# Grouped-query layer: four weight subtractions ordered behind the norm's last root, and the first attention pair written ahead of the second query projection

## The chip, the cores and the metric

The kernel runs on one core of a Trainium2 chip. The metric is the device time of one execution in microseconds (us). Before the change it is 1528.57 us, the median of three runs (1526.31 to 1530.88).

## The reference, cut to what matters

Two blocks follow one another on 256 tokens of width 1024, all in float32. The first block is two hybrid layers. The second is two transformer layers with a mixture of experts each; its first layer uses neighbourhood attention, its second grouped-query attention with 16 query heads and 4 key/value heads of width 64. The change touches the border between the two layers of the second block and the attention of the second:

```python
for i in range(DEPTH):                       # DEPTH = 2
    sh1, sc1, g1, sh2, sc2, g2 = split(silu(c) @ ada_w[i] + ada_b[i])
    h = x * (1 + sc1) + sh1
    y = neighbourhood_mixer(...) if i == 0 else gqa_mixer(h, ...)
    x = layer_norm(ALPHA * x + (1 + g1) * y, ln_g[i, 0], ln_b[i, 0])
    h = x * (1 + sc2) + sh2
    y = hierarchical_moe(h, ...)             # 32 experts
    x = layer_norm(ALPHA * x + (1 + g2) * y, ln_g[i, 1], ln_b[i, 1])

# gqa_mixer
qkv = h @ w_qkv                              # 1024 x (1024 + 256 + 256)
q, k = rope(rms_norm(q)), rope(rms_norm(k))
o = softmax(q @ k.T * HEAD_DIM**-0.5) @ v    # per head
return o @ w_o
```

## The kernel before, in words

The 256 tokens are two tiles of 128 partitions. A projection multiplies in float32 by splitting both operands into a high part and a remainder: `split` (L116) casts a piece of the weight to the high part on ScalarE (`S.copy`, L124) and subtracts it on VectorE (L125), 1024 columns at a time, and `mm3` (L172) issues three matmuls, high by high, low by high and high by low (L174). A 512-column weight slice takes four casts and four subtractions. Two such split slices of 256 columns are held at a time. In `proj_wide` (L311) with a `feed`, `feed(0)` writes the transposed, scaled activations of token tile 0, the weight is split, and the matmuls of tile 0 run; then `feed(1)` and tile 1. `feeder` (L278) makes one `feed`: per half of the width four transposes of x (L156), four scaled copies out of PSUM that alternate between VectorE (L221) and ScalarE (L227), one cast (L289) and one subtraction (L290).

At the end of the first mixture of experts (`moe` with l = 0, L1216 to L1220), each token tile is normalized: `norm_stats` (L748) takes `bn_stats` of the two halves (L754), the aggregate (L755), and an inverse square root out of small one-column VectorE steps (`rsqrt1`, L202, lines L205 to L209), and ends with L758, the bias of the normalization. `normalize` (L761) then writes the right half of x on ScalarE (L762) and the left half on VectorE (L763), both from PSUM. The 512 key and value columns (`wkv`) of the grouped-query layer have been loaded by then, and their splits need nothing of the norm.

`gqa_layer` (L880) is written in this order: load `wkv` and the first query columns `wq0`; project keys and values (L944, with the feed); load the second query columns `wq1`; project `wq0` (L948); `chain` for the keys (norm and rotation, L949); transpose keys; `chain` for query heads 0 to 7 (L957); project `wq1` (L958); `q_trans(0)`, the transposes of query heads 0 to 7 (L959); `chain` for heads 8 to 15 (L960); load the rows of the expert norm (`ln_rows`); and the loop over eight pairs of heads (L966), with `q_trans(1)` after pair 1 and the affine part of the norm (`affine`, L825) after pairs 3 and 5. `full_heads` (L389) of a pair is: scores into PSUM (tag pd, L393), maximum on VectorE (L345), four exponentials on ScalarE (L356), scaling by the sums (L219, L225), transposes (L156), copies (L217, L223), the product with the values (L398) and the split of the result (L836, L837). Pairs 0 to 3 need query heads 0 to 7 only. Between all this `ada` loads the modulation weights in chunks of 2 MB (L702) and multiplies them (L711, tile pf, 16 records a chunk); block 9 holds one of these chunks first and the softmax tiles later. After the loop come the last chunks, `flush`, and `mixer_out` (L765), whose weights `w_o` are split by the same helper.

PSUM tiles of tag pd (projections and scores) have two buffers, of tag ps three. Weights go through three rotating SBUF blocks; SP issues the loads in its own queue, each when its block is free.

The order of instructions on each engine is fixed when the program is built. A planner plays the program on a simulated timeline, and gives each engine, of the instructions that are ready there, the one written earliest. So the written order is a priority and not the order of execution. `tc.issue_after(i)` adds an edge of order alone: what is traced inside it on the engine of i is queued behind i.

Of the kernel before, what the change touches and what calls it, by code (L numbers as in the profile page):

```python
# [31 lines left out]
def tile_hybrid_then_moe(ctx: ExitStack, tc: tile.TileContext, p: dict, out: bass.AP):  # L32
# [33 lines left out]
    def block(i, dt=F32):  # L66
        i = role.get(i, i)
        t = big[i].tile([128, 4096], dt, name=f"b{i}", tag=f"b{i}")
        return t
# [20 lines left out]
    def cyc(vs):  # L90
        i = [0]

        def nxt():
            i[0] += 1
            return vs[(i[0] - 1) % len(vs)]
        return nxt
# [15 lines left out]
    def splitter():  # L112
        hs, ls = block(3, F32R), block(4, F32R)
        par = [0]

        def split(v):  # L116
            k, n = v.shape[1], v.shape[2]
            o = par[0] * 2048
            par[0] ^= 1
            hi, lo = [a[:, o:o + k * n].rearrange("p (k n) -> p k n", k=k) for a in (hs, ls)]  # L120
            step = max(1, 1024 // n)
            for a in range(0, k, step):
                s = slice(a, min(a + step, k))
                S.copy(hi[:, s], v[:, s])  # L124
                V.tensor_tensor(lo[:, s], v[:, s], hi[:, s].bitcast(F32), OP.subtract)  # L125
            return [(hi[:, a], lo[:, a]) for a in range(k)]
        return split

# [3 lines left out]
    def pair(i):  # L132
        return carve(block(i, F32R), (8, 256), (8, 256))
# [174 lines left out]
                    k == 0, k == 7)  # L308
        return ps.rearrange("p (f t) -> p f t", f=2)

    def proj_wide(h, split, v, feed=None, rest=None, ahead=()):  # L311
        o = PS2()
        if feed:
            feed(0)
            if rest:
                rest()
            with ExitStack() as q:
                for i in ahead:
                    q.enter_context(tc.issue_after(i))
                s = [(a, split(v[:, :, a:min(a + 256, v.shape[2])]))  # L320
                     for a in range(0, v.shape[2], 256)]
            for t in range(2):
                if t:
                    feed(1)
                for a, w in s:
                    proj_tok(h, w, t, o[:, t, a:min(a + 256, v.shape[2])])
            return o
        for a in range(0, v.shape[2], 256):
            n = min(256, v.shape[2] - a)
            s = split(v[:, :, a:a + n])  # L330
            for t in range(2):
                proj_tok(h, s, t, o[:, t, a:a + n])
        return o
# [414 lines left out]
    def norm_stats(src):  # L748
        n = len(src)
        st = small([128, n, 6], f"lst{n}")  # L750
        mv = small([128, 2], "lmv")
        rr = small([128, 2], "lrr")
        for i, v in enumerate(src):
            V.bn_stats(st[:, i], v)  # L754
        V.bn_aggr(mv, st)  # L755
        V.tensor_scalar(rr[:, 1:2], mv[:, 1:2], 1e-5, None, op0=OP.add)
        rsqrt1(rr[:, 0:1], rr[:, 1:2])
        V.tensor_scalar(rr[:, 1:2], mv[:, 0:1], rr[:, 0:1], -1.0, op0=OP.mult, op1=OP.mult)  # L758
        return mv, rr

    def normalize(t, src, mv, rr):  # L761
        S.activation(x[:, t, 512:D], src[1], AF.Identity, scale=rr[:, 0:1], bias=rr[:, 1:2])  # L762
        V.tensor_scalar(x[:, t, 0:512], src[0], mv[:, 0:1], rr[:, 0:1], op0=OP.subtract, op1=OP.mult)  # L763

    def mixer_out(split, l, y, w_o):  # L765
# [114 lines left out]
    def gqa_layer(l, split):  # L880
# [20 lines left out]
        def chain(pw, h0, n, qk):  # L901
            pv = pw[:, :, :n * 64].rearrange("p t (h d) -> p t h d", h=n)
            q = qs[:, :, :n]
            S.activation(q, pv, AF.Square)
            V.tensor_reduce(ssq[:, :, h0:h0 + n], q, AX.X, OP.add)
            rt = small([128, 2, n], f"rt{n}")
            rstd(rt, ssq[:, :, h0:h0 + n], 1e-6, (ALL, 1.0 / 64))
            if qk == 0:
                S.copy(q, pv)
                V.tensor_scalar(rs8[:, h0:h0 + n], rt.rearrange("p t h -> p h t"), 0.125, None, op0=OP.mult)  # L910
            else:
                V.tensor_tensor(q, pv, rt[:, :, :, None].to_broadcast([128, 2, n, 64]), OP.mult)
                S.copy(vv, pw[:, :, 256:512])
            for t in range(2):
                xv = q[:, t].rearrange("p h (a b r) -> p h a b r", a=2, b=2)
                tb = [tab[:, qk, t, i][:, None].to_broadcast([128, n, 2, 16]) for i in range(4)]
                tm = [ro[:, i, :n] for i in range(4)]
                V.tensor_tensor(tm[0], xv[:, :, :, 0], tb[0], OP.mult)
                V.tensor_tensor(tm[1], xv[:, :, :, 1], tb[1], OP.mult)
                V.tensor_tensor(tm[2], xv[:, :, :, 1], tb[2], OP.mult)  # L920
                V.tensor_tensor(tm[3], xv[:, :, :, 0], tb[3], OP.mult)
                for d in ([qk_t[:, t]] if qk == 0 else [kdup[:, t, :, dd] for dd in range(2)]):
                    d = d.rearrange("p h (a b r) -> p h a b r", a=2, b=2)
                    V.tensor_tensor(d[:, :, :, 0], tm[0], tm[1], OP.subtract)
                    V.tensor_tensor(d[:, :, :, 1], tm[2], tm[3], OP.add)

        def q_trans(half):
            for hp in range(2):
                ps = PS()
                for j in range(2):  # L930
                    for t in range(2):
                        hh = 4 * hp + 2 * j
                        tr(ps[:, j * 256 + t * 128:j * 256 + t * 128 + 128],
                           qk_t[:, t, hh:hh + 2].rearrange("p h d -> p (h d)"))
                evac(qT[:, 4 * half + 2 * hp:4 * half + 2 * hp + 2].rearrange("p h t -> p (h t)"), ps)
# [5 lines left out]
            pin[0] = False  # L941
            ada()

        pkv = proj_wide(hT, split, wkv, feed, rest)  # L944
        ada()
        wq1 = cols(wq, 512, 512)
        ada()
# [2 lines left out]
        for hp in range(2):  # L950
# [4 lines left out]
                       kdup[:, t, 2 * hp + j].rearrange("p c d -> p (c d)"))  # L955
            evac(kT[:, 2 * hp:2 * hp + 2].rearrange("p h t -> p (h t)"), ps)
        chain(pq, 0, 8, 0)  # L957
        pq = proj_wide(hT, split, wq1)  # L958
        q_trans(0)  # L959
        chain(pq, 8, 8, 0)  # L960
        lgb = carve(b10[:, 1024:3072], (D,), (D,))
        ln_rows(lgb, 0, 1)
        oT = pair(6)
        s0, s1, t0, t1 = carve(block(9), *[(2, 512)] * 4)
        bufs = (cyc([s0, s1]), cyc([t0, t1]))
        for hp in range(8):  # L966
            kv = hp // 2
            full_heads(bufs, qT[:, hp], kT[:, kv], lambda j: vv[:, :, kv * 64:kv * 64 + 64],
                       rs8[:, 2 * hp:2 * hp + 2], None, put_o(oT, hp))
            if hp == 1:  # L970
                q_trans(1)
            if hp in (3, 5):
                affine(lgb, V, (hp // 4,))
        adab[0] = cyc([7, 2])
        ada(48)
        flush()
# [4 lines left out]
    def moe(l, w1, lg, fs, fb, new):  # L981
# [234 lines left out]
        if not l:  # L1216
            for t in range(2):
                ys = [Y[t][:, 0], Y[t][:, 1]]
                normalize(t, ys, *norm_stats(ys))
            return  # L1220
        st, mv, rr, nm = carve(P.rearrange("p t e s -> p (t e s)"), (2, 2, 6), (2, 2), (2,), (1,))
        h = [slice(0, 512), slice(512, D)]
# [148 lines left out]
```

## Time and profile before

| | us |
|---|---|
| median of three runs | 1528.57 |
| the profiled execution | 1528.28 |
| its span, first to last instruction | 1526.4 |
| TensorE busy (PE) | 1213.0 (79%) |
| VectorE busy (DVE) | 576.3 (38%) |
| ScalarE busy (ACT) | 352.5 (23%) |
| DMA | 532.20 MB, mean 349 GB/s |

Times in the trace count from the span's start. PE is the matmul stream of TensorE, PEld its weight loads, SPq the queue of DMA issues. In a timeline row stand the start, the length, engine, line, operation, output and input tiles, count, and in brackets how long the engine had been idle and what released it. The table of stretches gives busy time per engine, then the granted clock of TensorE as a share of full speed, and the share of the DMA engines' time in use.

### The profile page before, as it was taken

To read this page: it belongs to the slowest core of one execution; us is meant where nothing else is said; L and a number is where in the kernel's file an instruction comes from. 1 tells how busy PE (TensorE), PEld (TensorE's weight loads), DVE (VectorE), ACT (ScalarE), POOL (GpSimd) and SP (SyncE) were. 2 spreads that over 40 slices of the span, in tenths; PEclk is the share of its full clock that TensorE was granted. 3 is DMA by queue.
4 is the path that set the end of the run, shared out by engine and by line. 5 is a ranking of instruction groups with operands and counts; after the bars stand their busy time and mean duration, and the time that the engine had idled before them with its cause. 6 is when DMAs were issued, how large, how long until landed. Compare 5 with 4: busy or idle time off the path is not lost.

```text
span 1526.4 us, 23782 instructions
## 1 busy us (share of the span) xinstructions
PE 1213.0 (79%) x10200; PEld 763.6 (50%) x10200; DVE 576.3 (38%) x1383; ACT 352.5 (23%) x747; POOL 47.9 (3%) x83
## 2 busy tenths in 40 slices
PE   6999899999998896672886677898897774596765
PEld 6887788786766442321432325657443321243322
DVE  6885687556566210100110106867311100011103
ACT  5443445345441010000010004562011000011000
POOL 0000000000000200000000000000300000000000
PEclk9999899999989998876998889899899977799788
DMA  9538444768477999999999999775999999999995
GB/s 360 219 124 336 173 157 159 297 259 349 184 282 291 429 430 430 429 429 430 430 429 430 430 428 381 280 276 212 378 428 431 428 429 430 430 428 430 430 430 211
DMA packets 46557, 532.20 MB, mean 349 GB/s; under 512 B 7024, under 2 KB 10224, under 8 KB 14960
## 3 DMA queue, kind: packets, MB, share of 16 engines
q1 hardware_dynamic: 45296, 527.48, 83.7%
q10 hardware_dynamic: 1152, 3.15, 0.5%
q8 instruction: 82, 1.34, 0.3%
q14 instruction: 27, 0.22, 0.0%
HBM read 529.56 MB, written 1.05 MB: 348 GB/s over the span
## 4 chain that ended last, share of the span: by engine, by line
DMA 46%; PE 43%; DVE 7%; ACT 3%; issue 1%; SPq 0%; DVEq 0%; ACTq 0%
DMA b<-in_moe_w_gate_up_dram 27%; DMA b<-in_moe_w_down_dram 17%; PE ps L159 13%; PE ps L174 11%; PE pd L174 11%; PE pd L159 3%; PE pf L159 3%; PE ps L156 2%; DVE b L125 2%; DMA b<-in_na_bias_dram 1%; ACT b L356 1%; ACT b L124 1%; DMA b<-in_w_in_dram 1%; DVE diag L744 0%; DVE b L868 0%
## 5 line engine op out<-in xcount | busy, mean ns | idle before, releaser
L159 PE MATMUL ps<-b,b 128*32 128x256 f32 (+2 forms) x5248 | 483.3, 476 | 191.0 <-DMA b<-in_moe_w_gate_up_dram 127.1
L159 PEld LDWEIGHTS ps<-b,b 128*32 128x32 f32 (+1 forms) x5248 | 191.5, 120 | 428.8 <-issue 270.1
L174 PE MATMUL ps<-b,b 128*128 128x256 f32 (+1 forms) x1464 | 195.4, 293 | 1.5 <-DVE b L125 1.3
L174 PE MATMUL pd<-b,b 128*128 128x256 f32 (+2 forms) x1152 | 188.0, 321 | 5.7 <-DVE b L464 4.0
L174 PEld LDWEIGHTS ps<-b,b 128*128 128x128 f32 x1464 | 183.9, 192 | 12.1 <-issue 3.2
L174 PEld LDWEIGHTS pd<-b,b 128*128 128x128 f32 x1152 | 163.4, 197 | 31.5 <-issue 7.1
L125 DVE TENSOR_TENSOR b<-b,b 128x1024 fp32r<-128x1024 f32 (+1 forms) x124 | 148.6, 1207 | 74.8 <-ACT b L124 74.3
L124 ACT CAST b<-b 128x1024 fp32r<-128x1024 f32 (+1 forms) x124 | 126.5, 1035 | 152.7 <-PE ps L174 68.9
L223 ACT COPY b<-ps 128x256 f32<-128x256 f32 (+1 forms) x81 | 36.0, 448 | 451.3 <-PE ps L159 305.9
L217 DVE COPY b<-ps 128x256 f32<-128x256 f32 (+1 forms) x71 | 36.1, 508 | 238.1 <-PE ps L159 201.3
L156 PE MATMUL ps<-cst,b 128*128 128x128 f32 (+1 forms) x404 | 76.1, 299 | 41.3 <-DVE b L217 17.5
L1087 DVE SCALAR_TENSOR_TENSOR sl<-sl,ps 128x128 f32<-128x128 f32 x64 | 18.4, 288 | 236.8 <-ACT sl L1086 236.8
L156 PEld LDWEIGHTS ps<-cst,b 128*128 128x128 f32 (+1 forms) x404 | 44.6, 145 | 108.0 <-DVE b L217 34.4
L1135 DVE TENSOR_TENSOR b<-ps,parts 128x512 f32<-128x512 f32 x32 | 22.1, 691 | 190.6 <-PE ps L159 189.5
L159 PE MATMUL pd<-b 64*128 64x512 f32 (+1 forms) x384 | 82.7, 553 | 13.2 <-DVE b L1135 8.3
L159 PEld LDWEIGHTS ps<-b,x 128*128 128x128 f32 x512 | 62.8, 202 | 20.8 <-issue 15.7
L159 PE MATMUL ps<-b,x 128*128 128x128 f32 x512 | 67.1, 290 | 3.7 <-DVE b L1101 1.6
L1086 ACT ACTIVATE sl<-ps 128x128 f32<-128x128 f32 x64 | 17.7, 277 | 222.9 <-PE ps L156 222.9
L1105 POOL TENSOR_TENSOR b<-b,g 128x128 f32<-128x128 f32 x64 | 23.5, 399 | 1249.1 <-DVE b L1101 730.8
L159 PEld LDWEIGHTS pd<-b 64*128 64x128 f32 x384 | 34.6, 192 | 50.1 <-issue 24.0
L227 ACT ACTIVATE b<-ps,modc 128x128 f32<-128x128 f32 x64 | 29.0, 457 | 125.1 <-DVE b L221 70.5
L159 PE MATMUL pf<-b,cz 128*32 128x512 f32 x384 | 54.0, 620 | 3.7 <-DMA b<-in_ada_w_dram 3.7
(287 smaller groups left out, 787.7 us busy)
## 6 DMA issues: line engine op xcount, KB each, us to landing
b<-in_moe_w_gate_up_dram SPq DMA_DIRECT2D x128, 2048.0 KB, 29.9
b<-in_moe_w_down_dram SPq DMA_DIRECT2D x62, 2048.0 KB, 32.1
b<-in_ada_w_dram SPq DMA_DIRECT2D x24, 2048.0 KB, 8.9
b<-in_w_in_dram SPq DMA_DIRECT2D x12, 2048.0 KB, 9.7
b<-in_na_w_qkv_dram SPq DMA_DIRECT2D x6, 2048.0 KB, 7.8
b<-in_gqa_w_qkv_dram SPq DMA_DIRECT2D x3, 2048.0 KB, 25.3
b<-in_w_out_dram SPq DMA_DIRECT2D x4, 1024.0 KB, 4.9
b<-in_w_out_dram SPq DMA_DIRECT2D x2, 2048.0 KB, 8.9
```

Of the source, the lines that this page charges most:

```text
L124: S.copy(hi[:, s], v[:, s])
L125: V.tensor_tensor(lo[:, s], v[:, s], hi[:, s].bitcast(F32), OP.subtract)
L156: T.transpose(o, a, ident)
L159: return T.matmul(o, lhsT=a, rhs=b, start=start, stop=stop)
L174: T.matmul(o, lhsT=a[u], rhs=b[v], start=start and i == 0, stop=stop and i == 2)
L217: V.tensor_copy(o, i)
L223: S.copy(o, i)
L227: S.activation(o, i, AF.Identity, scale=scale, bias=bias)
L1086: S.activation(sl, ps[:, 0:128], AF.Tanh, scale=0.5)
L1087: V.scalar_tensor_tensor(sl, sl, 1.0, ps[:, 0:128], op0=OP.add, op1=OP.mult)
L1105: G.tensor_tensor(PG[:, t, :, du].rearrange("p q (e s) -> p q e s", e=2), P[:, t].rearrange("p (q e) s -> p q e s", q=2), g32[:, t, 4 * g: ...
L1135: V.tensor_tensor(do, ps, parts, OP.mult)
```

## The change

The four subtractions of `wkv`'s split are queued behind the last L758 that `norm_stats` has traced (that of token tile 1). At the end of the first layer's experts, both halves of x are normalized on ScalarE. In `gqa_layer`, `q_trans(0)` and head pair 0 are written in front of the projection of `wq1`, pair 1 behind it, and `chain` of heads 8 to 15 after that; `q_trans(1)` follows pair 2, and the affine part follows pairs 4 and 6.

```diff
-        def split(v):
+        def split(v, hold=()):
...
                 S.copy(hi[:, s], v[:, s])
-                V.tensor_tensor(lo[:, s], v[:, s], hi[:, s].bitcast(F32), OP.subtract)
+                with ExitStack() as q:
+                    for i in hold:
+                        q.enter_context(tc.issue_after(i))
+                    V.tensor_tensor(lo[:, s], v[:, s], hi[:, s].bitcast(F32), OP.subtract)
...
-    def proj_wide(h, split, v, feed=None, rest=None, ahead=()):
+    def proj_wide(h, split, v, feed=None, rest=None, ahead=(), hold=()):
...
-                s = [(a, split(v[:, :, a:min(a + 256, v.shape[2])]))
+                s = [(a, split(v[:, :, a:min(a + 256, v.shape[2])], hold))
...
-        V.tensor_scalar(rr[:, 1:2], mv[:, 0:1], rr[:, 0:1], -1.0, op0=OP.mult, op1=OP.mult)
+        root[0] = V.tensor_scalar(rr[:, 1:2], mv[:, 0:1], rr[:, 0:1], -1.0, op0=OP.mult, op1=OP.mult).ins
         return mv, rr
 
-    def normalize(t, src, mv, rr):
+    root = [None]
+
+    def normalize(t, src, mv, rr, both=False):
         S.activation(x[:, t, 512:D], src[1], AF.Identity, scale=rr[:, 0:1], bias=rr[:, 1:2])
+        if both:
+            S.activation(x[:, t, 0:512], src[0], AF.Identity, scale=rr[:, 0:1], bias=rr[:, 1:2])
+            return
         V.tensor_scalar(x[:, t, 0:512], src[0], mv[:, 0:1], rr[:, 0:1], op0=OP.subtract, op1=OP.mult)
...
-        pkv = proj_wide(hT, split, wkv, feed, rest)
+        pkv = proj_wide(hT, split, wkv, feed, rest, hold=(root[0],))
...
         chain(pq, 0, 8, 0)
+        q_trans(0)
+        oT = pair(6)
+        s0, s1, t0, t1 = carve(block(9), *[(2, 512)] * 4)
+        bufs = (cyc([s0, s1]), cyc([t0, t1]))
+
+        def head(hp):
+            kv = hp // 2
+            full_heads(bufs, qT[:, hp], kT[:, kv], lambda j: vv[:, :, kv * 64:kv * 64 + 64],
+                       rs8[:, 2 * hp:2 * hp + 2], None, put_o(oT, hp))
+
+        head(0)
         pq = proj_wide(hT, split, wq1)
-        q_trans(0)
+        head(1)
         chain(pq, 8, 8, 0)
         lgb = carve(b10[:, 1024:3072], (D,), (D,))
         ln_rows(lgb, 0, 1)
-        oT = pair(6)
-        s0, s1, t0, t1 = carve(block(9), *[(2, 512)] * 4)
-        bufs = (cyc([s0, s1]), cyc([t0, t1]))
-        for hp in range(8):
-            kv = hp // 2
-            full_heads(bufs, qT[:, hp], kT[:, kv], lambda j: vv[:, :, kv * 64:kv * 64 + 64],
-                       rs8[:, 2 * hp:2 * hp + 2], None, put_o(oT, hp))
-            if hp == 1:
-                q_trans(1)
-            if hp in (3, 5):
-                affine(lgb, V, (hp // 4,))
+        head(2)
+        q_trans(1)
+        for hp in range(3, 8):
+            head(hp)
+            if hp in (4, 6):
+                affine(lgb, V, (hp // 6,))
...
-                normalize(t, ys, *norm_stats(ys))
+                normalize(t, ys, *norm_stats(ys), both=True)
```

## Rows read from the trace of the kernel before

**Rows 1.** The page: its span, and section 4, the chain by engine.

```profile
span 1526.4 us, 23782 instructions
...
DMA 46%; PE 43%; DVE 7%; ACT 3%; issue 1%; SPq 0%; DVEq 0%; ACTq 0%
```

**Rows 2.** The chain that ended last, in order of time: start, us, what.

```profile
935.69 5.93 PE pd L174 x48
...
950.17 12.45 PE pd L174 x104
...
1130.14 21.51 DMA b<-in_moe_w_down_dram
```

**Rows 3.** Stretches: us; PE, PEld, DVE, ACT, POOL busy; PEclk; DMA share; GB/s.

```profile
919.60:929.90 10.30, 2.81 (x22) 0.56 (x18) 10.08 (x30) 2.16 (x3) 0.00 (x0) 0.89 1.00 429
929.90:935.70 5.80, 3.87 (x18) 3.12 (x18) 3.78 (x8) 3.53 (x8) 0.00 (x0) 0.60 0.99 424
935.70:977.70 42.00, 42.00 (x343) 36.30 (x343) 29.43 (x75) 18.04 (x23) 0.00 (x0) 1.00 0.80 323
977.70:994.20 16.50, 11.79 (x62) 5.26 (x60) 16.33 (x43) 9.74 (x24) 0.00 (x0) 0.69 0.64 208
994.20:1032.20 38.00, 36.57 (x244) 21.62 (x243) 22.07 (x48) 25.45 (x77) 0.00 (x0) 1.00 0.70 270
1032.20:1088.00 55.80, 48.39 (x355) 39.45 (x354) 37.96 (x121) 11.56 (x22) 1.47 (x4) 0.88 0.67 262
...
1130.00:1500.00 370.00, 258.00 (x2558) 116.66 (x2550) 45.33 (x118) 26.44 (x73) 11.03 (x27) 0.86 1.01 429
```

**Rows 4.** Groups of instructions by form, VectorE, 919.6 to 929.9.

```profile
L125 DVE TENSOR_TENSOR b<-b,b 128x1024 fp32r<-128x1024 f32 x4 | 4.8, 1217 | 0.0
```

**Rows 5.** The timeline from the first root's end to the first dense matmuls.

```profile
929.02 0.20 DVE L758 TENSOR_SCALAR lrr<-lmv,lrr 128x1 f32<-128x1 f32 x1
...
929.32 1.46 ACT L762 ACTIVATE x<-pd,lrr 128x512 f32<-128x512 f32 x2 [8.14 <-DVE lrr L758]
...
930.13 1.53 DVE L763 TENSOR_SCALAR x<-pd,lmv,lrr 128x512 f32<-128x512 f32 x2 [0.22 <-ACT x L762]
...
931.00 2.82 PE L156 MATMUL ps<-cst,x 128*128 128x128 f32 x12 [6.82 <-DVE x L763]
932.15 0.41 DVE L221 TENSOR_SCALAR b<-ps,fs,fb 128x128 f32<-128x128 f32 x1 [0.49 <-PE ps L156]
...
934.94 0.69 DVE L290 TENSOR_TENSOR b<-b,b 128x512 fp32r<-128x512 f32 x1 [0.59 <-ACT b L289]
```

**Rows 6.** DMA issues between 927.9 and 929.0: KB each, us to landing.

```profile
b<-in_ada_w_dram SPq DMA_DIRECT2D x1, 2048.0 KB, 23.4
```

**Rows 7.** The timeline of the second query projection and the first pairs.

```profile
966.02 1.93 PE L159 MATMUL pf<-b,cz 128*32 128x512 f32 x16
...
968.77 1.06 ACT L124 CAST b<-b 128x1024 fp32r<-128x1024 f32 x1 [2.20 <-PE pd L174]
...
971.78 0.42 DVE L925 TENSOR_TENSOR b<-b 128x256 f32<-128x256 f32 x1
...
977.81 1.04 PE L156 MATMUL ps<-cst,b 128*128 128x128 f32 x8
...
979.53 1.13 PE L159 MATMUL pd<-b 64*128 64x256 f32 x8 [0.69 <-DVE b L217]
...
982.74 2.08 PE L159 MATMUL pd<-b 64*128 64x256 f32 x8 [2.08 <-ACT b L909]
...
984.42 0.56 ACT L356 ACTIVATE b<-pd,mx,rs 128x256 f32<-128x256 f32 x1 [1.73 <-DVE mx L352]
...
988.77 5.47 PE L159 MATMUL pf<-b,cz 128*32 128x512 f32 x26
```

**Rows 8.** Groups of instructions by form, VectorE, 974 to 992.

```profile
L345 DVE TENSOR_REDUCE mx<-pd 128x4 f32<-128x1024 f32 x3 | 3.6, 1215 | 0.0
L125 DVE TENSOR_TENSOR b<-b,b 128x1024 fp32r<-128x1024 f32 x2 | 2.4, 1220 | 3.3 <-ACT b L124 3.3
```

## Prediction, made blind

> **What bounds the kernel now.** The first view is the page: a span of 1526.4 us, and a chain of which DMA has 46% and TensorE 43% [rows 1]. The chain in order of time says where each holds. Through the border of the two layers and the whole grouped-query attention it runs on TensorE and on what releases it; from 1130 on it is the loading of expert weights [rows 2]. The stretches put numbers to that: from 1130 to 1500 the DMA share is 1.01, but from 929.9 to 1088 it lies between 0.64 and 0.99, and at 0.64 to 0.80 from 935.7 on [rows 3]. There the loads wait for blocks that the compute frees. So a microsecond saved before 1088 lets every later load start a microsecond earlier, and I count it fully to the end.
>
> Two holes are to be seen in these stretches. In the first, 919.6 to 929.9, VectorE is busy 10.08 of 10.30 us while TensorE does 2.81, and in the 5.80 us behind it the granted clock is 0.60 [rows 3]. In the second, 977.7 to 994.2, TensorE is busy 11.79 of 16.50 us at a clock of 0.69. Between them it works 42.00 of 42.00 at clock 1.00, and after the second 36.57 of 38.00.
>
> **The held subtractions.** In the first hole VectorE's queue mixes the two tiles' roots with four subtractions of `wkv`, 4.8 us in all [rows 4]. They are not needed until the third matmul of the projection. Held, they leave the roots 4.8 us earlier: the first L758, which ends at 929.22 [rows 5], at about 924.4, the second at about 925.1.
>
> From the first L758 to the dense projection at 935.69 [rows 2] it is 6.5 us now. What changes inside these: the normalization is two pieces on ScalarE at 0.73 us beside two on VectorE at 0.77 [rows 5]; it becomes four on ScalarE, 2.9 us, of which the first two, tile 0, are ready after 1.5 us instead of 1.7. ScalarE's first scaled copy can't begin before the fourth, some 0.5 us later than now, counted from the root. VectorE now has the subtractions in the same place: 4.8 us, and the copies of `feed(0)`, four of 0.41 and two subtractions of 0.69 [rows 5], or 3.0. The planner prefers `feed(0)`, which is written earlier, so I expect one or two subtractions ahead of its first copy, 1.2 to 2.4 us, mostly in time in which x isn't ready yet. On the other side the twelve transposes take 2.82 us at a falling clock [rows 5], 0.235 each, against 0.13 later (1.04 for eight [rows 7]); with a shorter pause part of that 1.2 us comes back.
>
> The bounds: at best the lead is 4.8 and the transposes' 1.2, less 0.1, so 5.9 us. At worst all four subtractions go first, until 929.9, and from VectorE's first copy to the dense start it takes the 3.5 us of now (932.15 to 935.69): 933.4, a lead of 2.3. Even with the subtractions last of all VectorE is through at 925.1 + 4.8 + 3.0 = 932.9. I take 4.5, near the lead itself.
>
> The row on the normalization says that ScalarE and VectorE cost the same here, 0.73 against 0.77 [rows 5]. The Trainium skill (ScalarE: Activation LUTs, "Rules for kernel authors") says to put multiplications and additions on VectorE, since ScalarE is slower; from its page's formula such an instruction of 512 elements with scale and bias as operands would take an estimated 0.80 us, four of them 3.2, and the gain would be 4.2. The row decides, and the two sums hardly differ.
>
> The shift goes through the 42 us of dense TensorE work if the data is there. The loads that could be late are SP's: `w_o` waits for the block that the last subtraction frees, up to 5 us later, and a modulation chunk issued behind it lands 23.4 us after its issue [rows 6], now at 951.4, then at 956 at the latest. TensorE multiplies it at 966.02 [rows 7], or 961.5 when shifted. It holds, so this delay costs nothing; without that margin it would cost up to 5 us. The cast of `w_o` at 968.77 comes later still.
>
> **The first pair in front.** Query heads 0 to 7 are ready when the last L925 ends at 972.2, but their transposes run at 977.81, after the whole second projection [rows 7]. Then come the scores of pair 0 at 979.53, and TensorE pauses for its maximum and exponentials, while VectorE is also busy with the second `chain`: 16.33 of 16.50 us [rows 3]. With `q_trans(0)` and pair 0 written ahead, the planner puts the transposes at about 972.3 to 974 (a modulation chunk of 1.93 us competes) and the scores of pair 0 some 6 us earlier than now, with about 31 matmuls of the projection left to cover its softmax. VectorE has the time: it idles 3.3 us in front of a `w_o` subtraction just there [rows 8].
>
> What can be won is the hole. TensorE's idle time in it is 16.50 - 11.79 = 4.7 us. The slow clock costs 0.95 on the pair at 982.74 (2.08 against 1.13), as much again on the pair after it, of the same length, and 5.47 - 26 x 0.12 = 2.35 on 26 modulation records [rows 7], where 0.12 is 1.93/16: 4.25. Together 8.95, the upper bound. The added operations are none; the same ones change places. Lower bound: VectorE stays full. Pairs 0 and 1 each need 1.22 us of maximum [rows 8] and about as much again in small steps, now ahead of the second `chain`, so that `chain` ends 4 to 5 us later; the pairs that wait for it, 4 to 7, are hidden behind pairs 1 to 3 as long as TensorE has those to do. If they are not, the hole only moves, and the gain is nothing; the case beyond is the rival below. VectorE's free 3.3 us is the nearest row for what can be moved up, and some clock comes back with it: I take 4 of the 8.95.
>
> The affine rows move by one pair, out of the way of nothing: they are needed by `mixer_out` alone, and VectorE is busy 22.07 of 38.00 us there [rows 3]. `ln_rows` waits for the second `chain`, so its two loads are issued later; they have the same pairs to land in.
>
> Sum: -4.5 - 4 = -8.5 against the profiled execution's 1528.28, so 1519.8; the median is 1528.57, 0.3 above it, and I say 1520.
>
> **Rivals.** (1) *The hole moves.* Pair 0 is done early, but the second `chain`, delayed by pairs 0 and 1, opens the same hole ahead of pair 4. For it speaks VectorE's 16.33 of 16.50; against it, pairs 2 and 3, which need no second chain. Only the held subtractions count: 1523.8.
>
> (2) *Less than half.* The subtractions land in front of `feed(0)` (gain 2.3) and the hole moves: 1526.
>
> (3) *Slower: TensorE's queue stands behind pair 0.* If the planner's timeline sees the queries ready too early, the transposes stand ahead of the projection's matmuls. TensorE then waits from the end of the first projection, 950.17 + 12.45 = 962.6 [rows 2], to 972.2 for the rotation: 9.6 us, unless other work stands in front of it there. If the second hole also stays, because the `chain` of the late projection follows as far behind, it is +9.6 - 4.5: 1533.4. It is slower than no change by 0.3% from 9.1 us of such waiting on. That a queue behaves so shows in the second hole, where the modulation matmuls of 988.77 stand behind the scores and wait with them. Against it: the planner doesn't keep the written order; `w_o`'s cast, written after the attention, runs at 968.77, ahead of `q_trans(0)` [rows 7], and in the dense 42 us its plan fits the chip without a gap.
> The Trainium skill (TensorE: Matmul & The Clock Gate, "Step-by-step: what each phase is for") says that matmuls stay in program order and only weight loads are pulled ahead; by that rule a misplaced transpose would hold up all matmuls behind it, and the trace agrees: TensorE is idle for 2.08 us before the scores at 982.74.
>
> **How the numbers follow.** 0.3% is 4.6 us, about what a measurement of this kernel can tell from no change. Forecast 0.58 (faster 0.55, same 0.03); rival 1 0.20, which lies at the limit (faster 0.09, same 0.11); rival 2 0.10 (same 0.08, slower 0.02 with some loss elsewhere); rival 3 0.12, slower. That is faster 0.64, same 0.22, slower 0.14. The range begins where both upper bounds hold, 1528.3 - 5.9 - 8.95 = 1513.4, and ends at 1530, which takes in rivals 1 and 2 and a small loss and leaves rival 3 out.
>
> **What would show it.** Right: no L125 between L754 and the last L758; the dense projection starting near 931; the transposes of `q_trans(0)` between matmuls of the second projection; the first exponential at about 973 instead of 984.42 [rows 7]; less idle time and a clock nearer to 1.00 in the 16 us behind the projection; the loads from 1130 on shifted by the sum. Wrong: an idle TensorE in the middle of the second projection, a modulation chunk that TensorE waits for, or the same pause ahead of pair 4.

## The result, and the profile after

The changed kernel is slower: 1534.07 us, median of 5 runs (1532.26 to 1537.61), against 1528.22 of the kernel before (5 runs, 1524.71 to 1530.88). The ratio is 1.0053, 95% interval [1.0033, 1.0073], so some 8 us by the ratio (the two medians lie 5.9 apart). The forecast was 1520.0, and the range ended at 1530. The profiled execution took 1532.26 us.

The page after, its span and the chain by engine, answers to [rows 1]:

```profile
span 1530.2 us, 23784 instructions
...
PE 45%; DMA 43%; DVE 8%; ACT 2%; issue 1%; SPq 0%; DVEq 0%; ACTq 0%
```

TensorE now holds more of the chain than DMA does. Line numbers moved by a few: the cast of a split is still L124, its subtraction is L128 (L125 before), the split matmuls are L177 (L174), transposes L159 (L156), other matmuls L162 (L159), the last step of a root L761 (L758), the scaled copies of `feed` L224 on VectorE and L230 on ScalarE (L221 and L227).

Single executions reach the border of the layers up to 5 us apart, although nothing ahead of it was changed. So positions are counted from the first cast of `wkv` on ScalarE, at 917.29 before and at 913.07 after. Each number below is the start (or end) of a row of one profiled execution less the start of that cast; the bottom six lines belong to the experiments. One execution can lie some us off the median of its kernel; where that bears on a reading, it is said there.

| | dense start | 2nd projection ends | last pair's split ends | 2nd gather starts | end of span |
|---|---|---|---|---|---|
| before | 17.67 | 60.68 | 116.01 | 156.40 | 609.11 |
| after | 15.25 | 71.36 | 127.39 | 164.45 | 617.13 |
| hold alone | 15.22 | 60.22 | 114.12 | 150.00 | 602.69 |
| order alone | 17.78 | 73.32 | 129.86 | 167.27 | 619.80 |
| scores in the other tag | 14.41 | 59.08 | 117.11 | 156.35 | 609.20 |
| hold in the gaps | 12.71 | 56.39 | 111.17 | 147.05 | 599.69 |
| hold without ScalarE | 17.56 | 60.45 | 116.12 | 156.86 | 609.84 |
| pair 0 inside the projection | 12.67 | 55.36 | 112.59 | 150.84 | 603.50 |

("Dense start" is the first matmul of the key and value projection, "gather" the first matmul of the second mixture of experts that reads x.) The change wins 2.4 us at the first mark, loses 13.1 between the first and the second, and gets 3.3 back between the third and the fourth. What stands at the gather, 8.05, stands at the end, 8.02: from there on the loading of weights passes any shift on, as [rows 3] had let expect.

**Where the loss is.** The stretches after, with the columns of [rows 3]:

```profile
925.70:928.30 2.60, 0.74 (x4) 0.75 (x5) 1.56 (x6) 2.03 (x5) 0.00 (x0) 0.50 1.06 454
928.30:957.80 29.50, 29.45 (x228) 25.03 (x227) 18.96 (x45) 13.08 (x19) 0.00 (x0) 0.96 0.89 372
957.80:970.75 12.95, 6.90 (x40) 2.80 (x39) 9.45 (x29) 3.08 (x4) 0.00 (x0) 0.74 0.82 324
970.75:984.45 13.70, 13.70 (x116) 12.90 (x114) 6.88 (x10) 7.21 (x16) 0.00 (x0) 1.00 0.00 1
984.45:1003.10 18.65, 14.60 (x88) 6.34 (x88) 14.50 (x43) 11.97 (x34) 0.00 (x0) 0.73 0.84 338
...
1134.00:1500.00 366.00, 258.12 (x2528) 118.34 (x2520) 44.33 (x115) 26.20 (x72) 11.04 (x27) 0.86 1.01 429
```

Before, TensorE worked without a break through both query projections, 42.00 of 42.00 us [rows 3]. Now a hole of 12.95 us with 6.90 of work lies between them (third line), and the hole behind the second projection, which the change was to fill, is there as well (fifth line, clock 0.73). The first line shows the clock at 0.50 in the pause ahead of the dense start, the last a DMA share of 1.01 as before. TensorE's own timeline says what it waits for; it answers to [rows 7]:

```profile
957.36 0.39 PE L177 MATMUL pd<-b,b 128*128 128x256 f32 x1
957.58 1.04 PE L159 MATMUL ps<-cst,b 128*128 128x128 f32 x8
964.22 0.69 PE L159 MATMUL ps<-cst,b 128*128 128x128 f32 x2 [5.60 <-DVE b L933]
964.84 3.59 PE L162 MATMUL pf<-b,cz 128*32 128x512 f32 x16
968.36 0.88 PE L159 MATMUL ps<-cst,b 128*128 128x128 f32 x6
969.69 1.14 PE L162 MATMUL pd<-b 64*128 64x256 f32 x8 [0.46 <-DVE b L220]
970.75 7.45 PE L177 MATMUL pd<-b,b 128*128 128x256 f32 x61
```

The first query projection ends at 957.75. After the key transposes TensorE is idle for 5.60 us, until VectorE's L933 has rotated the first token tile of query heads 0 to 7. Then come the query transposes, a modulation chunk at 3.59 us where it takes 1.93 at full clock [rows 7], and the scores of pair 0. Only behind these scores does the first of the 96 matmuls of the second projection run. Of the 12.95 us, 5.14 are work at its full-clock price (1.04 and 1.04 of transposes, 1.93, 1.13, prices of [rows 7]); 7.8 are lost.

Is it a buffer that is still in use? The last reader of tag pd ahead of the scores is ScalarE's copy of the first query projection:

```profile
960.84 1.01 ACT L917 COPY b<-pd 128x1024 f32<-128x1024 f32 x1 [1.56 <-DVE ssg L913]
```

From 961.85 on both buffers have been read out, 8.9 us ahead of the first matmul of the second projection. So on the chip at most the time up to 961.85 is a wait for a buffer. After that the projection stands where the planner has put it in TensorE's queue: behind the waiting transposes and the scores.

**At the border**, the rows that answer to [rows 5]:

```profile
920.32 0.20 DVE L761 TENSOR_SCALAR lrr<-lmv,lrr 128x1 f32<-128x1 f32 x1
...
920.62 0.78 ACT L767 ACTIVATE x<-pd,lrr 128x512 f32<-128x512 f32 x1 [3.67 <-DVE lrr L761]
...
921.13 4.62 DVE L128 TENSOR_TENSOR b<-b,b 128x1024 fp32r<-128x1024 f32 x4
...
925.67 0.72 DVE L224 TENSOR_SCALAR b<-ps,fs,fb 128x128 f32<-128x128 f32 x2
...
926.11 1.39 ACT L230 ACTIVATE b<-ps,fb,fs 128x128 f32<-128x128 f32 x3 [2.70 <-DVE b L224]
...
928.32 7.31 PE L177 MATMUL pd<-b,b 128*128 128x256 f32 x49
```

The first root ends 7.45 us behind the cast, instead of 11.93. But all four held subtractions run in one piece in front of the first copy of `feed(0)`, and ScalarE's copy waits 2.70 us for that one.

### The profile page after: what moved, and what is told of

It is laid out like the page before. It is cut to its first block, busy times and chain, and to the rows that moved or that the text cites. A ratio compares the mean times of both kernels' runs of the same rounds, so it can differ in the third digit from the quotient of the medians.

```text
span 1530.2 us, 23784 instructions
## 1 busy us (share of the span) xinstructions
PE 1215.3 (79%) x10200; PEld 765.5 (50%) x10200; DVE 575.1 (38%) x1381; ACT 354.6 (23%) x749; POOL 47.9 (3%) x83
## 4 chain that ended last, share of the span: by engine, by line
PE 45%; DMA 43%; DVE 8%; ACT 2%; issue 1%; SPq 0%; DVEq 0%; ACTq 0%
DMA b<-in_moe_w_gate_up_dram 26%; DMA b<-in_moe_w_down_dram 15%; PE ps L162 14%; PE pd L177 11%; PE ps L177 11%; PE pd L162 3%; PE ps L159 3%; PE pf L162 2%; DVE b L128 2%; DMA b<-in_gqa_w_qkv_dram 2%; DMA b<-in_na_bias_dram 1%; ACT b L124 1%; ACT b L359 1%; DVE b L220 1%; DMA b<-in_w_in_dram 0%
## 5 line engine op out<-in xcount | busy, mean ns | idle before, releaser
L162 PE MATMUL ps<-b,b 128*32 128x256 f32 (+2 forms) x5248 | 484.3, 476 | 188.8 <-DMA b<-in_moe_w_gate_up_dram 127.8
L162 PEld LDWEIGHTS ps<-b,b 128*32 128x32 f32 (+1 forms) x5248 | 192.2, 120 | 426.5 <-issue 270.7
L177 PE MATMUL ps<-b,b 128*128 128x256 f32 (+1 forms) x1464 | 193.8, 291 | 1.5 <-DVE b L128 1.3
L177 PE MATMUL pd<-b,b 128*128 128x256 f32 (+2 forms) x1152 | 187.7, 321 | 5.4 <-DVE b L467 4.2
L177 PEld LDWEIGHTS ps<-b,b 128*128 128x128 f32 x1464 | 182.8, 191 | 11.7 <-issue 3.2
L177 PEld LDWEIGHTS pd<-b,b 128*128 128x128 f32 x1152 | 162.9, 197 | 30.7 <-issue 6.6
L128 DVE TENSOR_TENSOR b<-b,b 128x1024 fp32r<-128x1024 f32 (+1 forms) x124 | 148.5, 1208 | 79.0 <-ACT b L124 77.0
L124 ACT CAST b<-b 128x1024 fp32r<-128x1024 f32 (+1 forms) x124 | 126.5, 1035 | 147.4 <-PE ps L177 68.8
L159 PE MATMUL ps<-cst,b 128*128 128x128 f32 (+1 forms) x404 | 77.2, 302 | 48.6 <-DVE b L220 17.5
L159 PEld LDWEIGHTS ps<-cst,b 128*128 128x128 f32 (+1 forms) x404 | 45.1, 146 | 116.2 <-ACT b L226 34.2
L162 PE MATMUL pd<-b 64*128 64x512 f32 (+1 forms) x384 | 83.5, 559 | 14.1 <-DVE b L1149 8.4
L162 PEld LDWEIGHTS ps<-b,x 128*128 128x128 f32 x512 | 67.5, 215 | 21.4 <-issue 16.3
L162 PE MATMUL ps<-b,x 128*128 128x128 f32 x512 | 71.7, 303 | 3.4 <-DVE b L1115 1.6
L162 PEld LDWEIGHTS pd<-b 64*128 64x128 f32 x384 | 34.9, 194 | 51.2 <-issue 24.0
L230 ACT ACTIVATE b<-ps,modc 128x128 f32<-128x128 f32 x64 | 29.1, 458 | 131.1 <-DVE b L224 75.0
L162 PE MATMUL pf<-b,cz 128*32 128x512 f32 x384 | 53.9, 629 | 3.7 <-DMA b<-in_ada_w_dram 3.7
```

The lines of the kernel that those rows point to most:

```text
L159: T.transpose(o, a, ident)
L162: return T.matmul(o, lhsT=a, rhs=b, start=start, stop=stop)
L177: T.matmul(o, lhsT=a[u], rhs=b[v], start=start and i == 0, stop=stop and i == 2)
L230: S.activation(o, i, AF.Identity, scale=scale, bias=bias)
```

## Experiments

The theory after these rows: the hold gains about what its lower bound said; the order loses because in the plan the second projection gets no PSUM tile until pair 0's scores have been issued (both use tag pd, two buffers, and the planner seems to hand them out in written order). The rivals: the transposes alone stand in the way (TensorE's order, whatever the tiles), or the loss belongs to the hold, through a late load.

**Hold alone.** The change without its new order; the loop over pairs is that of before.

```diff
-        q_trans(0)
...
-        head(0)
         pq = proj_wide(hT, split, wq1)
-        head(1)
+        q_trans(0)
         chain(pq, 8, 8, 0)
```

> Held subtractions and both halves of x on ScalarE, the attention written as before. From the start of wkv's cast to the end of the last pair's split it is 116.0 us before and 127.4 us after the change; to the first dense matmul of the projection 18.4 and 15.9. Theory 1 (the loss comes from the attention's new order, the hold gains about 2.5 us): 15.9 to the dense matmuls, 113 to 114 to the last split, ratio 0.998. Rival (the hold delays something further on, for instance w_o's load or a modulation chunk): 116 or more to the last split, ratio 1.000 to 1.005.

Measured: 1523.62 us (12 runs) against 1527.36 (29 runs), ratio 0.9975 [0.996, 0.999]. The hold gains 3.8 us by the ratio, near theory 1's 0.998. The table shows that this isn't simply its lead: 2.45 us at the dense start are 0.46 at the end of the second projection, 1.9 at the last pair and 6.4 at the gather. The profiled execution took 1520.08, 3.5 below the median, so this 6.4 isn't the typical gain. The last section comes back to that.

**Order alone.** The change without the hold and with the left half of x on VectorE.

```diff
-        pkv = proj_wide(hT, split, wkv, feed, rest, hold=(root[0],))
+        pkv = proj_wide(hT, split, wkv, feed, rest)
-                normalize(t, ys, *norm_stats(ys), both=True)
+                normalize(t, ys, *norm_stats(ys))
```

> The attention's new order alone, no hold, x normalized as before. Theory 1: the second projection starts only behind pair 0's scores, 9 to 12 us later than before; 129 to 131 us from wkv's cast to the last split, ratio 1.006 to 1.008. Rival (the loss needs both parts): 116 to 120, ratio 1.000 to 1.003.

Measured: 1537.8 us, ratio 1.0077 [1.0054, 1.01]. By the ratio that is +11.8 us, and the hold's -3.8 beside it makes +8.0, the loss of the whole change (by the medians +10.4 and -3.7, beside 5.9). The two parts add within the intervals, and the loss is the order's.

**Scores in the other tag.** The change, but pair 0's scores take two tiles of tag ps. The written order is untouched.

```diff
-        s = PS2()
+        s = [PS(), PS()] if two else PS2()
```

> The changed kernel with pair 0's scores in two PSUM tiles of tag ps instead of one of tag pd (its maximum is then two reductions of half the width). Theory 1a (PSUM tiles of tag pd are given out in the order in which their first writes are written, so the second projection can have none until pair 0's scores are issued): the second projection starts at once behind the first, no 5.6 us of idle TensorE, and the last split comes 110 to 116 us after wkv's cast, ratio 0.994 to 1.000. Rival 1b (VectorE: pair 0 and the chains are too much for it in this place, wherever the projection stands): the projection starts early, but the last split stays at 122 to 128 us, ratio 1.003 to 1.006. Rival 1c (the planner prefers pair 0 by its priority): order and time as in the changed kernel.

Measured: 1527.44 us, ratio 1.0004 [0.9991, 1.0018]. TensorE between the projections:

```profile
961.49 0.38 PE L159 MATMUL ps<-cst,b 128*128 128x128 f32 x2
961.63 1.07 PE L177 MATMUL pd<-b,b 128*128 128x256 f32 x7
962.54 0.82 PE L159 MATMUL ps<-cst,b 128*128 128x128 f32 x6
963.12 7.20 PE L177 MATMUL pd<-b,b 128*128 128x256 f32 x59
...
976.71 1.14 PE L162 MATMUL ps<-b 64*128 64x256 f32 x8
```

With another tag for the scores the idle time between the projections is gone, with the same written order. So it is the shared tag that puts the projection behind the scores, and the scores still come behind it, at 976.71. The last split (117.11, expected 110 to 116) and the ratio lie just outside what theory 1a said. And this version only reaches the kernel before: with the hold in it, it should have reached the hold alone, 3.8 us lower, if pair 0 in front cost nothing.

**Pair 0 behind the projection.** The change with only `q_trans(0)` left in front.

```diff
         q_trans(0)
-        head(0)
         pq = proj_wide(hT, split, wq1)
+        head(0)
         head(1)
```

> The changed kernel with pair 0 behind the second projection again, only the transposes of query heads 0 to 7 stay in front of it. Theory 1a: the transposes need no tile of tag pd, so the projection starts at once, and the transposes run inside it; 109 to 114 us from wkv's cast to the last split, ratio 0.994 to 0.998. Rival 1c (anything written in front holds the projection up until the queries are rotated): 122 us or more, ratio 1.003 to 1.006.

Measured: 1525.45 us, ratio 0.9994 [0.9979, 1.0008]. The transposes alone, written in front, hold nothing up:

```profile
960.10 0.39 PE L177 MATMUL pd<-b,b 128*128 128x256 f32 x1
960.33 0.38 PE L159 MATMUL ps<-cst,b 128*128 128x128 f32 x2
960.47 1.07 PE L177 MATMUL pd<-b,b 128*128 128x256 f32 x7
```

The first line is the last matmul of the first query projection, which ends at 960.49, the third the start of the second, at 960.47: no gap. The rival that the transposes stand in the way falls. The time is not what theory 1a said: the last split comes at 115.49 (109 to 114 expected), and the ratio misses 0.994 to 0.998. The 1.8 us between this median and that of the hold alone can't be told from nothing, since the two intervals overlap.

**Hold in the gaps.** The hold alone, its four subtractions placed one by one: the first behind the last root, the second behind the first subtraction of `feed(0)`, the others behind its second.

```diff
+            f0 = feed(0)
+            if hold:
+                hold = [hold[0], f0[0], f0[1], f0[1]]
...
-                    for i in hold:
-                        q.enter_context(tc.issue_after(i))
+                    if hold:
+                        q.enter_context(tc.issue_after(hold.pop(0)))
```

> The hold alone, but the four held subtractions placed one by one: the first behind the last root, the second behind feed(0)'s first subtraction, the third and fourth behind its second one. Theory (the four subtractions in one piece ahead of feed(0)'s copies took half of the lead): the dense start moves from 15.2 us behind wkv's cast to 13 to 14, VectorE's first copy of feed(0) no longer waits for 4.6 us of subtractions, and the time falls by 1 to 2.3 us against the hold alone, to 1521.5 to 1522.5 (before 1527.4). Rival: the projection's third matmul needs the held low part, so what feed(0) wins is lost again behind it: dense start 15 to 16, 1523.5 to 1524.5.

Measured: 1517.55 us (6 runs) against 1527.21 (29 runs), ratio 0.9941 [0.9923, 0.996]; faster than before, and by the medians 6 us faster than the hold alone, more than the 1 to 2.3 expected. (From the cast to the end the two profiled executions differ by 3.0 us only, 599.69 and 602.69.) Its border:

```profile
925.13 1.22 DVE L128 TENSOR_TENSOR b<-b,b 128x1024 fp32r<-128x1024 f32 x1
...
926.82 1.78 DVE L224 TENSOR_SCALAR b<-ps,fs,fb 128x128 f32<-128x128 f32 x4 [0.47 <-PE ps L159]
...
929.52 6.49 PE L177 MATMUL pd<-b,b 128*128 128x256 f32 x32
...
929.99 1.22 DVE L128 TENSOR_TENSOR b<-b,b 128x1024 fp32r<-128x1024 f32 x1
...
932.05 2.35 DVE L128 TENSOR_TENSOR b<-b,b 128x1024 fp32r<-128x1024 f32 x2
```

VectorE now waits for the transposes (0.47 us) instead of the other way round, and the dense start is at 12.71, 5.0 us earlier than before. The 32 first matmuls need 6.49 us, 0.20 each, at a granted clock of 0.55 from 931.81 to 934.81; before, the dense stretch ran at 1.00 throughout [rows 3]. Of this version's lead of 4.96 us, 4.29 are left at the end of the second projection.

**Hold without ScalarE.** The hold alone, the left half of x normalized on VectorE as before.

```diff
-                normalize(t, ys, *norm_stats(ys), both=True)
+                normalize(t, ys, *norm_stats(ys))
```

> The hold alone, with the left half of x normalized on VectorE as in the kernel before. Theory (the two engines cost the same for a 512-wide normalization, 0.73 against 0.77 us, so the move to ScalarE does nothing by itself): dense start within 0.5 us of the hold alone's 15.2, the time within 1 us of 1523.6. Rival: with the halves on VectorE, 1.5 us of its queue stand ahead of the held subtractions and of feed(0)'s copies: dense start 16 to 17, 1524.5 to 1525.5, that is, the ScalarE move is a part of the gain.

Measured: 1527.78 us, ratio 1.0006 [0.999, 1.0021]. The theory fell, and the rival had too small a size: without the move to ScalarE the hold gains nothing.

```profile
923.05 4.62 DVE L128 TENSOR_TENSOR b<-b,b 128x1024 fp32r<-128x1024 f32 x4
927.59 1.52 DVE L771 TENSOR_SCALAR x<-pd,lmv,lrr 128x512 f32<-128x512 f32 x2
...
928.45 2.82 PE L159 MATMUL ps<-cst,x 128*128 128x128 f32 x12 [6.62 <-DVE x L771]
```

The normalization of VectorE stands behind the held subtractions, which are released at the same root and were written earlier; the transposes then wait 6.62 us for x, as they waited 6.82 before [rows 5].

**ScalarE alone.** Only `both=True` added to the kernel before.

```diff
-                normalize(t, ys, *norm_stats(ys))
+                normalize(t, ys, *norm_stats(ys), both=True)
```

> Only the left halves of x moved to ScalarE; the four subtractions are not held, attention as before. Theory (the move is worth something only because held subtractions would otherwise stand in front of VectorE's normalization): without the hold there is nothing to get out of the way of, dense start 17 to 18 us behind wkv's cast as before, and the time within 1.5 us of before. Rival: the move is worth the 4.2 us by which the hold with it beats the hold without it, whatever else is done: dense start 15 to 16, 1523 to 1524.

Measured: 1527.08 us, ratio 1.0011 [0.9997, 1.0024], dense start 17.38. Neither of the two edits shows a gain alone; the gain is in the two together. (Counted from the cast, its one profiled execution ends 4.0 us later than that of before; the medians, 0.3 us apart, don't show that. In it TensorE waits 3.44 us for a modulation chunk at 998.23; in the trace of before it doesn't.)

**w_o behind the rotation.** The hold alone, with the first half of the subtractions of `w_o` held behind the `chain` of heads 8 to 15, to clear VectorE in the second hole.

```diff
-            w = split(v[:, 0:2]) + split(v[:, 2:4])
+            w = sum([split(v[:, a:a + 2], (qend,) if qend and not i else ()) for a in (0, 2)], [])
...
-        chain(pq, 8, 8, 0)
+        qend = chain(pq, 8, 8, 0)
```

> The hold alone, with the first half of w_o's subtractions held behind the rotation of heads 8 to 15. Theory (the hole behind the second projection is VectorE's: subtractions of 2 x 1.22 us stand between the maxima and the rotation that the later pairs need): the stretch from the projection's end to the last pair's split, 53.9 us in the hold alone, gets 1 to 2.4 us shorter, and the end comes as much earlier, at 1521 to 1522.5. Rival: the hole is made by the pair's own chain of maximum, exponential and transposes, and the subtractions sit in idle time of VectorE: 53.9 within 0.5, and 1523 to 1524.5; if w_o's block then comes free later and a load is late, 1 to 2 us slower.

Measured: 1527.93 us, ratio 1.001 [0.9995, 1.0024], 4.3 us above the hold alone. Both expectations missed: the stretch from the projection's end to the last split takes 60.89 us instead of 53.90, and the loss is larger than the late load that the rival allowed for:

```profile
977.05 0.69 DVE L220 COPY b<-ps 128x512 f32<-128x512 f32 x1 [5.78 <-PE ps L159]
...
986.53 1.22 DVE L128 TENSOR_TENSOR b<-b,b 128x1024 fp32r<-128x1024 f32 x1
...
987.75 3.49 DVE L128 TENSOR_TENSOR b<-b,b 128x1024 fp32r<-128x1024 f32 x3
991.16 0.60 DVE L222 TENSOR_SCALAR b<-b,sums 128x256 f32<-128x256 f32 x2
...
996.62 1.93 PE L162 MATMUL pf<-b,cz 128*32 128x512 f32 x8 [3.11 <-DMA b<-in_ada_w_dram]
```

In the hold alone these subtractions are through at 977.58, ahead of pair 0's maximum at 978.62. Held, they leave VectorE idle for 5.78 us and then run all four with one small step between, in front of the rescaling (L222) of a pair. TensorE also waits 3.11 us for a modulation chunk. That the later `w_o` is the cause of this wait isn't shown: in ScalarE alone, where nothing of `w_o` is held, one of 3.44 us stands in nearly the same place. As at the border, what is held until one event runs there almost in one piece.

**Both placements.** The two edits together.

```diff
+                hold = [hold[0], f0[0], f0[1], f0[1]]
...
+        qend = chain(pq, 8, 8, 0)
```

> Both placements, of the held subtractions and of w_o's. Theory: the two gains add, since one lies ahead of the dense stretch and one behind it: 2 to 4 us below the hold alone, 1519.5 to 1521.5. Rival: each is covered, and the time stays within 1 us of the hold alone's 1523.6.

Measured: 1523.27 us, ratio 0.998 [0.997, 0.9991]: about the first gain less the second loss. The theory missed, and the rival has the number but not the reason. The dense start is at 12.49, as in the gaps, and what it gives is lost again in the attention.

**Pair 0 inside the projection.** The hold in the gaps, and pair 0 written behind the first half of the second projection, so that the projection has its tile first; the rest in the order of the change.

```diff
-        head(0)
-        pq = proj_wide(hT, split, wq1)
+        q1(0)
+        head(0)
+        q1(256)
         head(1)
```

> On top of the held subtractions in the gaps (1517.55): pair 0 is written behind the first half of the second projection, so that the projection has its PSUM tile before the scores want one; the rest of the changed order as in the change. Theory (pair 0 in front gives nothing of its own: its scores wait for the rotation of heads 0 to 7, and its maximum and steps only join the work of VectorE that makes the hole): no idle TensorE between the two query projections, and 1516 to 1520. Rival (the gain of 4 us that the prediction counted exists, and only the late projection hid it): 1512 to 1514.5.

Measured: 1520.3 us, ratio 0.9961 [0.9948, 0.9973], beside 0.9941 [0.9923, 0.996] for the hold in the gaps: no gain, and 0.3 us above the theory's range.

```profile
957.72 6.36 PE L177 MATMUL pd<-b,b 128*128 128x256 f32 x52
...
968.79 0.82 PE L159 MATMUL ps<-cst,b 128*128 128x128 f32 x6
970.51 1.13 PE L162 MATMUL pd<-b 64*128 64x256 f32 x8 [0.91 <-DVE b L220]
```

TensorE has no hole between the projections, and still the scores of pair 0 come at 970.51, 1.56 us behind the end of the projection (968.95). They stand 1.56 us behind it in the hold in the gaps and in the kernel before as well. So this version didn't bring pair 0 into the projection; heads 0 to 7 are rotated only at 966.27, 2.7 us before it ends. What pair 0 under a projection is worth is to be read from the changed kernel instead, where it does run ahead: its first exponential starts at 972.38, with most of the projection to come. From the end of the projection to the last split that kernel takes 56.03 us and the order alone 56.54, with one pair less to do, against 55.33 before and 53.90 in the hold alone (third column of the table less the second). The 4 us that the prediction counted are in neither.

## Why the prediction was wrong

**What bounds the kernel.** Right: the shift at the second gather (8.05) is the shift of the end (8.02).

**The held subtractions, -4.5.** The mechanism was right, the size was not. The roots came 4.5 us earlier. The step that failed is "I expect one or two subtractions ahead of its first copy": there were four, since they are ready at the root and the copies of `feed(0)` only after the transposes. The dense start gained 2.4 us (or 3.2 from the dense 935.69 of [rows 2]); my lower bound, built on this very case, was 2.3. Placed in the gaps, they gained 5.0 of my upper bound of 5.9. A second sentence failed behind it: "The shift goes through the 42 us of dense TensorE work if the data is there". In the hold alone 2.45 us went in and 0.46 came out. Its first 16 matmuls took 4.18 us, 0.26 each at a granted clock of 0.50, which the pause before them had too, against 0.12 at full clock (48 in 5.93 [rows 2]); that is 2.2 us.

**ScalarE and VectorE at the same price.** The durations are equal (0.78 and 0.77 on ScalarE, 1.52 for two on VectorE), and from that I let the move count for 0.1 us of delay. But what stands ahead in the engine's queue decides: with the move the hold is worth 3.8 us, without it nothing. The Trainium skill (ScalarE: Activation LUTs, "Rules for kernel authors"), by which such work belongs on VectorE, would have chosen the slower version here; its reason, a VectorE up to three times as fast per element, is given for bf16, and in this float32 case the two take the same time.

**The delay on SP, 0.** The price was right, the path wasn't the one that I counted. The load of `w_o` is issued 2.4 us later, 12.70 us behind the cast instead of 10.30, but no chunk stands close behind it: the one that did before is issued ahead of it now, at 920.00 against 925.77, and TensorE multiplies it at 955.51 without a wait.

**Pair 0 in front, -4.** Wrong in sign. The sentence that failed is that "the planner puts the transposes at about 972.3 to 974", with "about 31 matmuls of the projection left to cover its softmax". All 96 ran behind the scores. I named the two buffers of tag pd ahead of the prediction and never counted who holds them. Rival 3 is what happened, for another reason than I gave (a planner that sees the queries ready too early): its 9.6 us of waiting measure 7.8 us lost in a hole of 12.95, and the order alone costs 11.8. That its 1533.4 lies so near to 1534.07 is in part luck, since its -4.5 for the hold was too much as well. I gave it 0.12, on the argument that the planner doesn't keep the written order. It doesn't keep that of instructions; it does, it seems, that of the first writes to a tag's buffers (the scores in the other tag and pair 0 behind the projection speak for it; the planner itself was not looked into). The Trainium skill's rule on program order (TensorE: Matmul & The Clock Gate, "Step-by-step: what each phase is for"), which I had weighed for this rival, agrees with the 5.60 us in which nothing passes the waiting transposes, though the modulation chunk behind them had landed at 953.1; but which instructions stand behind them was the planner's doing.

**The hole.** Rival 1 was right that it isn't filled (14.60 of 18.65 us at clock 0.73, against 11.79 of 16.50 at 0.69), but it didn't move ahead of pair 4: it stays behind the second projection. What it is made of I read too loosely, as a pause for pair 0's maximum and exponentials beside a full VectorE. Of its 4.71 us of idle time before, 2.08 lie ahead of pair 1's scores [rows 7] and 1.95 ahead of pair 2's:

```profile
986.76 2.08 PE L159 MATMUL pd<-b 64*128 64x256 f32 x8 [1.95 <-ACT b L356]
```

The releaser of the first wait, L909, is the copy that reads the second projection out of its pd tile, and pair 1's scores need none of its data; that of the second, L356, are the exponentials that read pair 0's scores. Both waits end when a tile of tag pd has been read out. So the hole, too, looks like a matter of the two buffers of tag pd. The scores in the other tag bear this out in part: with pair 0's scores out of the way, pair 1's run at 977.67 without a wait, and a wait for the copy (1.87 us) stands ahead of pair 2's instead. A version with the later pairs' scores in another tag was not run. In the 54 us behind the projection TensorE works 48.99 us in the gaps version and 46.61 with pair 0 inside the projection (sums of three stretches of 18 us); why is not shown.

**Open.** That the projection falls behind pair 0's scores through the tag that they share is shown by a change of tag and by one of order. That the planner hands tiles out by written order is a conclusion from this; how it chooses in other cases was not tried.

## What to carry to other kernels

Moving work forward in a planned order moves its claim on buffers too: count, for the tag it writes, who waits for a tile until the moved work has run. Work held behind one event came out almost in one piece at both places tried here, and stood in front of everything that became ready a moment later; place it piece by piece behind the work that is to go first. And price a move between engines by what it then no longer stands behind, not by the two durations alone.

## What the hardware showed that I had not expected

In the profiled executions half of the gain of the best version lies where nothing was changed, behind the attention. From the last pair's split to the second gather, the stretch of before and then that of the hold alone, with the columns of [rows 3]:

```profile
1033.30:1073.69 40.39, 34.19 (x187) 29.04 (x187) 33.60 (x110) 8.78 (x14) 0.00 (x0) 0.88 0.65 254
```

```profile
1028.93:1064.81 35.88, 29.85 (x183) 25.38 (x183) 32.48 (x104) 8.78 (x14) 0.00 (x0) 1.00 0.71 279
```

TensorE's idle time is the same, 6.20 and 6.03 us; its work takes 4.34 us less, at a granted clock of 1.00 in place of 0.88. The same twelve matmuls of the output projection in the two, before first:

```profile
1038.14 4.02 PE L174 MATMUL pd<-b,b 128*128 128x512 f32 x12
...
1053.54 4.58 PE L174 MATMUL ps<-b,b 128*128 128x512 f32 x12
```

```profile
1032.65 3.07 PE L177 MATMUL pd<-b,b 128*128 128x512 f32 x12
...
1047.05 3.03 PE L177 MATMUL ps<-b,b 128*128 128x512 f32 x12
```

The hold alone, the hold in the gaps and `w_o` behind the rotation keep 1.00 through this stretch and need 35.9 us for it; the other versions, the changed kernel with 37.06 among them, fall below it in some part and need up to 40.7. Of the 9.4 us by which the hold in the gaps ends earlier, 4.5 come from here. The 15 us in front of the stretch had a clock of 1.00 in both kernels, with 13.69 us of work before and 14.78 in the hold alone; but the changed kernel also had 14.78 and ran at 0.83 in the first 10 us of the stretch all the same. So what decides it is open. So is whether it belongs to a version or to single executions: there is one trace of each kernel, and the 12 executions of the hold alone reach from 1518.47 to 1525.29 us.
